# One of the eight shifted taps of the value tile's 3x3 convolution made by ScalarE and added by GpSimd, in a one-core Trainium2 block kernel

## The chip, the cores and the metric

The kernel runs on one core of one Trainium2 chip. The metric is the device time of one execution in microseconds (us). Three runs of the kernel before gave 1514.31, 1516.21 and 1516.56 us; the median is 1516.21 us.

Engines are named as in the profile: PE is TensorE's matmul, PEld its weight load, DVE is VectorE, ACT is ScalarE, POOL is GpSimd, SP is SyncE, whose queue issues the DMAs.

## What is computed

The block has two sub-layers on a latent stream of 1024 positions by 1024 channels (a grid of 16 rows by 64 columns). The first is a token mixer; the change does not touch it. The second is a convolutional feed-forward layer, and the change lies wholly in it:

```python
def dwconv2d(u, w, bias):
    c = u.shape[-1]
    y = lax.conv_general_dilated(u, w[:, :, None, :].astype(u.dtype), window_strides=(1, 1),
                                 padding="SAME", dimension_numbers=("NHWC", "HWIO", "NHWC"),
                                 feature_group_count=c)
    return y + bias

def conv_ffn(h, rows, w_up, conv_w, conv_b, w_down):
    b, n, _ = h.shape
    u = (h @ w_up).reshape(b, rows, n // rows, 2 * D_FF)
    u = dwconv2d(u, conv_w, conv_b).reshape(b, n, 2 * D_FF)
    gate, val = jnp.split(u, 2, axis=-1)
    return (jax.nn.gelu(gate) * val) @ w_down
```

D_FF is 2816, so the up-projection gives 22 tiles of 128 gate channels and 22 tiles of 128 value channels. Each channel is convolved over the grid with its own 3x3 weights: a centre tap and eight shifted taps.

## The kernel before

The order of the instructions on each engine is the order in which the program writes them; no scheduler changes it. Each engine works its own list in order, and semaphores make it wait for the others.

The feed-forward layer's first half is the loop of `ffn`, with one step for each n from 0 to 21. A step makes gate tile n and value tile n in PSUM, two tiles of 128x1024 called `ug` and `uv`, from seven products of half tiles (`up_product`, L1526, 12 matmuls of 128x512 each). The order of the products in step n is (n,0), then (n-1,6), then (n,1) to (n,5), so that a tile's last product, number 6, runs inside the next step. The four halves are the banks a0, a1 of `ug` and v0, v1 of `uv`. Between the products ScalarE moves banks (`copy`, L131): a0 to a1 after product 0 (`ug<-ug` in the profile), a1 to v0 after product 1 (`uv<-ug`), v1 to the buffer `p5` after product 3 (`p<-uv`), v0 to the buffer `u3` after product 5 (`u<-uv`). VectorE joins: a1 += p5 (`up_join` "g", L1542) and v1 += u3 (`up_join` "v", L1542, at the end of the step).

The convolution of a tile is `conv`: ScalarE writes the accumulator, centre tap and bias (L1552), and eight shifted taps are put in a queue. Each tap is one VectorE instruction (L1564) that reads the PSUM tile, multiplies with a weight per channel and adds into the accumulator in SBUF. Four of the eight taps (the corners) work on 15x63 = 945 elements, two on 960 and two on 1008. `up_conv(n-1, "v")` is called behind product (n-1,6), and the gate's behind join "g". VectorE's list for one step n is then: eight gate taps of tile n-1, five value taps of tile n-1, join "g" of n, three value taps of n-1, join "v" of n.

The weights of the next step are prepared in this step by `up_split`: ScalarE writes the rounded part (L131, `s<-s`), GpSimd the remainder (L138), one pair for each product. Splits 0 and 6 come first, then 1 and 2; behind split 2 GpSimd also makes a difference of weights (L1492), and then comes `glu(n-2)`, the product of gate and value tile (L1574), which is stored by DMA. Splits 3, 4 and 5, each with a sum of weights (L1474, L1476, L1478), end GpSimd's list of the step. ScalarE's list between splits 6 and 1 holds the value accumulator of tile n-1 and the copy `uv<-ug`.

`gate` (here `self.gp`) is a pool with four buffers of 128x512, tags `ghi`, `graw`, `glo` and `rb`. `p5` uses `ghi` and `graw` in turn, `u3` uses `glo` and `rb` in turn. After the loop, `down` does the down-projection (PE `dn`, L1795); the last tile's convolution lies in its first pass.

The loop's body, cut to the calls on which the steps below rest:

```python
for m, i in [(n, 0), (n - 1, 6)] + [(n, i) for i in range(1, 6)]:
    ...
                self.up_split(n + 1, i)
    ...
            if i == 0:
                self.taps(n - 1, "gt", 8)
            elif i == 6:
                self.up_conv(n - 1, "v")
            elif i == 2 and n > 1:
                self.glu(n - 2)
            elif i == 3:
                self.taps(n - 1, "vt", 5)
```

Of the kernel before, what the change touches and what calls it, by code (L numbers as in the profile page):

```python
# [8 lines left out]
F32 = mybir.dt.float32  # L9
F32R = mybir.dt.float32r  # L10
AF = mybir.ActivationFunctionType
OP = mybir.AluOpType
# [5 lines left out]
NP = FF // 128  # L18
# [94 lines left out]
class K:  # L113
# [1401 lines left out]
    def up_product(self, n, i):  # L1515
        nc, u = self.nc, self.U[n]
        name, form, b = self.PRODUCTS[i]
        w, (bh, bl) = u["w"].pop(name), self.B[form]
        o = self.bank(n, b)
        fresh = i in (0, 3)  # L1520
        for k in range(4):
            hi, lo = [w[:, j, k * 128:(k + 1) * 128] for j in range(2)]
            h, l = [x[k // 2][:, k % 2, :] for x in (bh, bl)]
            for m, (x, y) in enumerate(((hi, h), (hi, l), (lo, h))):
                first = fresh and k == 0 and m == 0
                nc.tensor.matmul(o, x, y, start=first, stop=k == 3 and m == 2, skip_group_check=not fresh)  # L1526
        self.sl.free(w)
        if i == 0:
            self.copy("act", self.bank(n, "a1"), o)
        elif i == 1:  # L1530
            self.copy("act", self.bank(n, "v0"), o)
        elif i == 3:
            u["p5"] = self.gp.tile([128, 512], F32, name="p5", tag=("ghi", "graw")[n % 2])
            self.copy("act", u["p5"], o)
        elif i == 5:
            u["u3"] = self.gp.tile([128, 512], F32, name="u3", tag=("glo", "rb")[n % 2])
            self.copy("act", u["u3"], o)

    def up_join(self, n, x):
# [3 lines left out]

    def up_conv(self, n, x):
        u = self.U[n]
        u[x + "a"], u[x + "t"] = self.conv(u[x], n if x == "g" else NP + n)

    def conv(self, ps, ti):

        nc = self.nc  # L1550
        acc = self.sl.get([128, S], any_=True)
        nc.scalar.activation(acc, ps, AF.Identity, bias=self.par["fcb"][:, ti:ti + 1], scale=self.fcw(4, ti))  # L1552
        a3 = acc.rearrange("p (y x) -> p y x", y=GH)
        p3 = ps.rearrange("p (y x) -> p y x", y=GH)
        taps = deque()
        for dy in (-1, 0, 1):
            for dx in (-1, 0, 1):
                if dy == 0 and dx == 0:
                    continue
                y0, y1, x0, x1 = max(0, -dy), GH - max(0, dy), max(0, -dx), GW - max(0, dx)  # L1560
                o = a3[:, y0:y1, x0:x1]
                i = p3[:, y0 + dy:y1 + dy, x0 + dx:x1 + dx]
                taps.append(lambda o=o, i=i, w=self.fcw((dy + 1) * 3 + dx + 1, ti):
                            nc.vector.scalar_tensor_tensor(o, i, w, o, op0=OP.mult, op1=OP.add))  # L1564
        return acc, taps

    def gelu(self, n):
        g = self.U[n]["ga"]
# [16 lines left out]
    def ffn(self):  # L1585
        sl = self.sl
        self.G = [self.dp.tile([128, 1024], F32, name=f"G{n}") for n in range(NP)]
        last = NP - 1

        todo = deque([(0, 4), (0, 5), (0, 6), (1, 1), (1, 3), (1, 4), (1, 5), (1, 6)])  # L1590
        self.down_plan()
        for n in range(NP):
            if n > 1:
                self.up_banks(n)
            if n + 2 < NP and n:
                self.up_load(n + 2)
            for m, i in [(n, 0), (n - 1, 6)] + [(n, i) for i in range(1, 6)]:
                if m >= 0 and not (n < 2 and i in (0, 2)):
                    if n == 0 or n == 1 and todo:
                        for _ in range(2 if n == 0 else 1):  # L1600
                            if todo:
                                self.up_split(*todo.popleft())
                    self.up_product(m, i)
                    if m == last:
                        self.up_free(i)
                if n == 0:
                    if i == 3:
                        self.up_load(2)
                    if i == 4:
                        self.up_join(0, "g")  # L1610
                        self.up_conv(0, "g")
                    continue
                if n + 1 < NP:
                    if n == 1 and i == 0:
                        self.up_sums(2)
                    self.up_split(n + 1, i)
                if n + 2 < NP and i in (3, 4, 5):
                    self.up_sums(n + 2, [i - 3])
                if i == 0:
                    self.taps(n - 1, "gt", 8)  # L1620
                elif i == 6:
                    self.up_conv(n - 1, "v")
                elif i == 2 and n > 1:
                    self.glu(n - 2)
                elif i == 3:
                    self.taps(n - 1, "vt", 5)
                elif i == 4:
                    self.gelu(n - 1)
                    self.up_join(n, "g")
                    self.up_conv(n, "g")  # L1630
                    self.taps(n - 1, "vt", 8)
            if n < last:
                self.up_join(n, "v")
        self.down()
# [362 lines left out]
```

## Time and profile before

| | |
|---|---|
| median of three runs | 1516.21 us |
| the profiled execution's own time | 1516.26 us |
| span of its trace | 1514.5 us |
| mean granted TensorE clock | 0.975 |
| PE busy | 1397.1 us (92%) |
| DVE busy | 1178.0 us (78%) |
| ACT busy | 668.7 us (44%) |
| POOL busy | 606.7 us (40%) |

The span is 1.8 us shorter than the profiled execution's own time. Busy shares are averages over stages that differ: the loop of `ffn` lies at 785 to 1275 us of the span, and its steady part is read in the rows below. In a timeline row the first number is the start in us from the span's start, the second the length, and the brackets hold the engine's idle time just before and what ended it.

### The profile page before, as it was taken

How to read it: one execution, taken by the hardware profiler on the slowest of the kernel's cores; microseconds unless marked ns; L12 is line 12 of the kernel's file. 1: busy time of each engine (PE TensorE's matmuls, PEld its weight loads, DVE VectorE, ACT ScalarE, POOL GpSimd, SP SyncE). 2: the span in 40 equal slices, each digit the busy share in tenths (PEclk: the TensorE clock that was granted, in tenths of full speed). 3: DMA queues.
4: the chain of work that ended last, by engine and by line, in shares of the span. 5: the costliest groups of instructions: out<-in, count | busy, mean ns of one | idle time of the engine just before them, and what ended most of it. 6: DMA issues, size and time to landing. Idle time of an engine off the chain costs nothing.

```text
span 1514.5 us, 16967 instructions
## 1 busy us (share of the span) xinstructions
PE 1397.1 (92%) x6333; PEld 1122.0 (74%) x6333; DVE 1178.0 (78%) x1347; ACT 668.7 (44%) x964; POOL 606.7 (40%) x422
## 2 busy tenths in 40 slices
PE   5999999998999689988995899999999999999994
PEld 3788888877888578877874677777777777788883
DVE  5768868767113988476567999999999999998696
ACT  6566677755110213332235444444444444545461
POOL 2221121122001443277057778777788775300000
PEclk9999999999999899999996999999999999999997
DMA  9310110101113445422431022211222208741642
GB/s 373 108 35 21 50 35 22 63 28 42 42 56 117 156 146 167 124 96 69 140 111 56 28 84 84 84 62 64 84 84 84 70 28 308 291 151 56 229 139 112
DMA packets 52787, 155.21 MB, mean 102 GB/s; under 512 B 5781, under 2 KB 10192, under 8 KB 52704
## 3 DMA queue, kind: packets, MB, share of 16 engines
q1 hardware_dynamic: 51264, 151.76, 28.7%
q10 hardware_dynamic: 1184, 2.11, 0.5%
q8 instruction: 50, 0.82, 0.2%
q14 instruction: 33, 0.27, 0.1%
q0 software_dynamic: 256, 0.25, 0.1%
HBM read 131.29 MB, written 22.81 MB: 102 GB/s over the span
## 4 chain that ended last, share of the span: by engine, by line
DVE 35%; PE 18%; issue 5%; ACT 1%; DMA 0%; DVEq 0%; ACTq 0%
DVE s L1564 24%; PE dn L1795 9%; PE big L194 6%; DVE s L138 2%; PE uv L1526 1%; PE ug L1526 1%; DVE ug L1542 1%; DVE uv L1542 1%; DVE s L1225 1%; DVE s L1787 1%; PE big L1212 0%; DVE s L1366 0%; DVE t L1367 0%; DVE s L338 0%; DVE s L1729 0%
## 5 line engine op out<-in xcount | busy, mean ns | idle before, releaser
L194 PE MATMUL big<-s,s 128*128 128x512 f32 (+2 forms) x2352 | 558.6, 396 | 9.0 <-DVE s L138 6.4
L194 PEld LDWEIGHTS big<-s,s 128*128 128x128 f32 (+2 forms) x2352 | 438.1, 189 | 114.2 <-DVE s L138 7.8
L138 POOL TENSOR_TENSOR s<-s,s 128x512 fp32r<-128x512 f32 (+1 forms) x229 | 351.3, 1551 | 273.2 <-ACT s L131 178.9
L131 ACT ACTIVATE s<-s 128x512 fp32r<-128x512 f32 (+2 forms) x406 | 264.4, 697 | 236.9 <-DVE mid L912 62.1
L1526 PE MATMUL ug<-s,s 128*128 128x512 f32 x1056 | 264.5, 399 | 24.3 <-ACT uv L131 13.4
L1526 PEld LDWEIGHTS ug<-s,s 128*128 128x128 f32 x1056 | 198.4, 190 | 79.5 <-ACT uv L131 22.0
L138 DVE TENSOR_TENSOR s<-s,s 128x512 fp32r<-128x512 f32 (+3 forms) x209 | 190.2, 940 | 74.3 <-ACT s L131 53.1
L1795 PE MATMUL dn<-s,s 128*128 128x512 f32 x924 | 216.3, 395 | 5.1 <-DVE s L138 4.0
L1564 DVE SCALAR_TENSOR_TENSOR s<-ug,rest,s 128x945 f32<-128x945 f32 (+2 forms) x176 | 214.9, 1221 | 5.4
L1564 DVE SCALAR_TENSOR_TENSOR s<-uv,rest,s 128x945 f32<-128x945 f32 (+2 forms) x176 | 214.7, 1220 | 4.7
L1526 PE MATMUL uv<-s,s 128*128 128x512 f32 x792 | 201.3, 404 | 11.3 <-DVE uv L1542 9.8
L1795 PEld LDWEIGHTS dn<-s,s 128*128 128x128 f32 x924 | 174.2, 189 | 46.9 <-DVE s L138 4.9
L1526 PEld LDWEIGHTS uv<-s,s 128*128 128x128 f32 x792 | 150.3, 192 | 54.8 <-DVE uv L1542 18.5
L782 POOL TENSOR_TENSOR s<-s,s 128x1280 f32<-128x1280 f32 x8 | 25.2, 3152 | 190.9 <-ACT s L778 190.9
L899 POOL TENSOR_TENSOR s<-s,s 128x1024 f32<-128x1024 f32 x8 | 21.1, 2642 | 127.4 <-PE big L194 120.7
L131 ACT ACTIVATE p<-uv 128x512 f32<-128x512 f32 x22 | 13.2, 600 | 106.2 <-PE uv L1526 106.2
L745 DVE SCALAR_TENSOR_TENSOR s<-big,par,s 128x1023 f32<-128x1023 f32 (+1 forms) x24 | 30.8, 1282 | 34.2 <-ACT s L742 33.6
L885 DVE TENSOR_TENSOR s<-big,s 128x1024 f32<-128x1024 f32 x8 | 9.8, 1223 | 61.1 <-PE big L194 61.1
L1574 POOL TENSOR_TENSOR s<-s,s 128x1024 f32<-128x1024 f32 x22 | 53.4, 2427 | 3.0 <-DVE s L1564 3.0
L1474 POOL TENSOR_TENSOR s<-s,s 128x512 f32<-128x512 f32 x22 | 28.6, 1299 | 63.5 <-DMA s<-in_ffn_w_up_b_dram 63.5
L1552 ACT ACTIVATE s<-uv,rest 128x1024 f32<-128x1024 f32 x22 | 26.6, 1208 | 47.6 <-POOL s L138 30.9
L777 ACT ACTIVATE s<-big,rest 128x1024 f32<-128x1024 f32 x32 | 35.7, 1117 | 24.6 <-PE big L194 17.8
(231 smaller groups left out, 1457.7 us busy)
## 6 DMA issues: line engine op xcount, KB each, us to landing
s<-in_mod_w_dram SPq DMA_DIRECT2D x48, 512.0 KB, 4.8
s<-in_ffn_w_up_b_dram SPq DMA_DIRECT2D x44, 512.0 KB, 4.4
s<-in_w_in_b_dram SPq DMA_DIRECT2D x32, 512.0 KB, 4.6
s<-G SPq DMA_DIRECT2D x55, 256.0 KB, 3.8
G<-s SPq DMA_DIRECT2D x22, 512.0 KB, 2.6
s<-in_ffn_w_down_dram SPq DMA_DIRECT2D x22, 512.0 KB, 7.1
s<-in_x_dram SPq DMA_DIRECT2D x16, 512.0 KB, 5.7
s<-G SPq DMA_DIRECT2D x11, 512.0 KB, 8.6
```

Of the source, the lines that this page charges most:

```text
L131: self.nc.scalar.activation(out, in_, AF.Copy)
L138: (self.nc.vector if eng == "dve" else self.nc.gpsimd).tensor_tensor(out, a, b, op=OP.subtract)
L194: return [lambda x=x: nc.tensor.matmul(x[0], x[1], x[2], start=x[3], stop=x[4]) for x in calls]
L745: nc.vector.scalar_tensor_tensor(u[:, lo:hi], z[:, lo + s:hi + s], tap[t], u[:, lo:hi], op0=OP.mult, op1=OP.add)
L777: nc.scalar.activation(lat, ps, AF.Sigmoid, bias=col)
L1474: p.tensor_tensor(u["x"][:, L], rg[:, L], rv[:, L], op=OP.subtract)
L1526: nc.tensor.matmul(o, x, y, start=first, stop=k == 3 and m == 2, skip_group_check=not fresh)
L1542: self.nc.vector.tensor_tensor(o, o, p, op=OP.add)
L1552: nc.scalar.activation(acc, ps, AF.Identity, bias=self.par["fcb"][:, ti:ti + 1], scale=self.fcw(4, ti))
L1564: nc.vector.scalar_tensor_tensor(o, i, w, o, op0=OP.mult, op1=OP.add))
L1574: nc.gpsimd.tensor_tensor(u["ga"], u["ga"], u["va"], op=OP.mult)
L1795: nc.tensor.matmul(bank[j], x, z, start=first and m == 0, stop=end and m == 2, skip_group_check=not check)
```

## The change

One of the eight value taps, the first corner (945 elements), leaves VectorE. In `conv`, for value tiles 0 to 20, ScalarE multiplies the shifted PSUM values with the tap's weight into two buffers `m` (8 rows of 63 = 504 elements and 7 rows of 63 = 441), right behind the accumulator. In `ffn`, at product (n,2), ahead of `glu(n-2)`, GpSimd adds the two buffers into the accumulator (L1635 in the changed file). VectorE's queue for the tile holds seven taps. The buffers `m` take the tags `graw` and `rb`; `p5` and `u3` keep one tag each. Tile 21 is not changed.

```diff
         elif i == 3:
-            u["p5"] = self.gp.tile([128, 512], F32, name="p5", tag=("ghi", "graw")[n % 2])
+            u["p5"] = self.gp.tile([128, 512], F32, name="p5", tag="ghi")
             self.copy("act", u["p5"], o)
         elif i == 5:
-            u["u3"] = self.gp.tile([128, 512], F32, name="u3", tag=("glo", "rb")[n % 2])
+            u["u3"] = self.gp.tile([128, 512], F32, name="u3", tag="glo")
             self.copy("act", u["u3"], o)
...
-        u[x + "a"], u[x + "t"] = self.conv(u[x], n if x == "g" else NP + n)
+        u[x + "a"], u[x + "t"], u[x + "r"] = self.conv(u[x], n if x == "g" else NP + n, x == "v" and n < NP - 1)
...
+                if shared and rest is None:
+                    rest = []
+                    h = (y1 - y0 + 1) // 2
+                    for tag, e in (("graw", slice(0, h)), ("rb", slice(h, y1 - y0))):
+                        m = self.gp.tile([128, 512], F32, name="m", tag=tag)
+                        m = m[:, 0:(min(e.stop, y1 - y0) - e.start) * (x1 - x0)].rearrange("p (y x) -> p y x", x=x1 - x0)
+                        nc.scalar.activation(m, i[:, e], AF.Copy, scale=self.fcw((dy + 1) * 3 + dx + 1, ti))
+                        rest.append((o[:, e], m))
+                    continue
...
-                elif i == 2 and n > 1:
-                    self.glu(n - 2)
+                elif i == 2:
+                    for o, m in self.U[n - 1]["vr"]:
+                        self.nc.gpsimd.tensor_tensor(o, o, m, op=OP.add)
+                    if n > 1:
+                        self.glu(n - 2)
```

GpSimd's list at product (n,2) of a step of the loop, before: two splits, the difference of weights, and the product of gate and value tile.

```order
L138 TENSOR_TENSOR s_6384<-s_6275,s_6384 128x512
L138 TENSOR_TENSOR s_6399<-s_6179,s_6399 128x512
L1492 TENSOR_TENSOR s_6179<-s_6179,s_6275 128x512
L1574 TENSOR_TENSOR s_6153<-s_6153,s_6222 128x1024
L138 TENSOR_TENSOR s_6419<-s_6181,s_6419 128x512
```

The same place with the change (line numbers are those of the changed file; `s_6384` is here the accumulator of value tile n-1):

```order
L138 TENSOR_TENSOR s_6403<-s_6291,s_6403 128x512
L138 TENSOR_TENSOR s_6418<-s_6189,s_6418 128x512
L1492 TENSOR_TENSOR s_6189<-s_6189,s_6291 128x512
L1635 TENSOR_TENSOR s_6384<-s_6384,m 128x8x63
L1635 TENSOR_TENSOR s_6384<-s_6384,m 128x7x63
L1584 TENSOR_TENSOR s_6164<-s_6164,s_6232 128x1024
L138 TENSOR_TENSOR s_6440<-s_6191,s_6440 128x512
```

The two adds stand behind the splits 1 and 2 and the difference of weights, and ahead of everything else of the step.

VectorE's list for the value taps of that tile, before, from the last gate tap of tile n-1 to the first gate tap of tile n:

```order
L1564 SCALAR_TENSOR_TENSOR s_6300<-ug,rest,s_6300 128x15x63
L1564 SCALAR_TENSOR_TENSOR s_6369<-uv,rest,s_6369 128x15x63
L1564 SCALAR_TENSOR_TENSOR s_6369<-uv,rest,s_6369 128x960
L1564 SCALAR_TENSOR_TENSOR s_6369<-uv,rest,s_6369 128x15x63
L1564 SCALAR_TENSOR_TENSOR s_6369<-uv,rest,s_6369 128x16x63 x2
L1542 TENSOR_TENSOR ug<-ug,p_6417 128x512
L1564 SCALAR_TENSOR_TENSOR s_6369<-uv,rest,s_6369 128x15x63
L1564 SCALAR_TENSOR_TENSOR s_6369<-uv,rest,s_6369 128x960
L1564 SCALAR_TENSOR_TENSOR s_6369<-uv,rest,s_6369 128x15x63
L1542 TENSOR_TENSOR uv<-uv,u_6464 128x512
L1564 SCALAR_TENSOR_TENSOR s_6447<-ug,rest,s_6447 128x15x63
```

And with the change:

```order
L1574 SCALAR_TENSOR_TENSOR s_6316<-ug,rest,s_6316 128x15x63
L1574 SCALAR_TENSOR_TENSOR s_6384<-uv,rest,s_6384 128x960
L1574 SCALAR_TENSOR_TENSOR s_6384<-uv,rest,s_6384 128x15x63
L1574 SCALAR_TENSOR_TENSOR s_6384<-uv,rest,s_6384 128x16x63 x2
L1574 SCALAR_TENSOR_TENSOR s_6384<-uv,rest,s_6384 128x15x63
L1542 TENSOR_TENSOR ug<-ug,p_6438 128x512
L1574 SCALAR_TENSOR_TENSOR s_6384<-uv,rest,s_6384 128x960
L1574 SCALAR_TENSOR_TENSOR s_6384<-uv,rest,s_6384 128x15x63
L1542 TENSOR_TENSOR uv<-uv,u_6484 128x512
L1574 SCALAR_TENSOR_TENSOR s_6468<-ug,rest,s_6468 128x15x63
```

The tap of 945 elements that stood first is gone; five value taps still stand ahead of join "g", two instead of three between the joins, and every one of them works on the accumulator into which GpSimd adds.

ScalarE's list around the copy `uv<-ug`, with the change:

```order
L1553 ACTIVATE s_6384<-uv,rest 128x1024
L1570 ACTIVATE m<-uv,rest 128x504
L1570 ACTIVATE m<-uv,rest 128x441
L131 ACTIVATE uv<-ug 128x512
L131 ACTIVATE s_6403<-s_6291 128x512
L131 ACTIVATE s_6418<-s_6189 128x512
```

The two rows L1570 are new; the others stand in the same order before.

## Rows read from the trace of the kernel before

**Rows 1.** The page, part 4: chain that ended last, shares by line.

```profile
DVE s L1564 24%; PE dn L1795 9%; PE big L194 6%; DVE s L138 2%; PE uv L1526 1%; PE ug L1526 1%; DVE ug L1542 1%; DVE uv L1542 1%; DVE s L1225 1%; DVE s L1787 1%; PE big L1212 0%; DVE s L1366 0%; DVE t L1367 0%; DVE s L338 0%; DVE s L1729 0%
```

**Rows 2.** Stretches: length; busy (x) of PE, PEld, DVE, ACT, POOL; granted clock; DMA.

```profile
1056.00:1076.90 20.90, 19.88 (x85) 15.62 (x84) 20.44 (x19) 9.36 (x14) 16.39 (x13) 1.00 0.21 76
```

**Rows 3.** Timeline of one step of the loop: VectorE.

```profile
1056.70 6.29 DVE L1564 SCALAR_TENSOR_TENSOR s<-uv,rest,s 128x945 f32<-128x945 f32 x5
1062.91 0.69 DVE L1542 TENSOR_TENSOR ug<-ug,p 128x512 f32<-128x512 f32 x1
1067.10 0.69 DVE L1542 TENSOR_TENSOR uv<-uv,u 128x512 f32<-128x512 f32 x1
1067.70 10.02 DVE L1564 SCALAR_TENSOR_TENSOR s<-ug,rest,s 128x945 f32<-128x945 f32 x8
```

**Rows 4.** The same step, in order of time: TensorE, ScalarE and GpSimd.

```profile
1056.59 1.29 POOL L1492 TENSOR_TENSOR s<-s,s 128x512 f32<-128x512 f32 x1
1057.84 2.42 POOL L1574 TENSOR_TENSOR s<-s,s 128x1024 f32<-128x1024 f32 x1
1059.30 0.60 ACT L131 ACTIVATE p<-uv 128x512 f32<-128x512 f32 x1 [4.90 <-PE uv L1526]
...
1067.85 3.06 PE L1526 MATMUL uv<-s,s 128*128 128x512 f32 x12 [0.35 <-DVE uv L1542]
1070.74 2.88 PE L1526 MATMUL ug<-s,s 128*128 128x512 f32 x12
1070.99 1.21 ACT L1552 ACTIVATE s<-uv,rest 128x1024 f32<-128x1024 f32 x1 [1.82 <-POOL s L138]
1073.66 0.58 ACT L131 ACTIVATE uv<-ug 128x512 f32<-128x512 f32 x1 [1.46 <-PE ug L1526]
1074.85 2.56 POOL L138 TENSOR_TENSOR s<-s,s 128x512 fp32r<-128x512 f32 x2 [3.57 <-ACT s L131]
1077.49 1.30 POOL L1492 TENSOR_TENSOR s<-s,s 128x512 f32<-128x512 f32 x1
```

**Rows 5.** Groups of 888 to 1265 us by form: busy, mean ns.

```profile
L1564 DVE SCALAR_TENSOR_TENSOR s<-uv,rest,s 128x945 f32<-128x945 f32 x72 | 86.2, 1197 | 1.3
L1574 POOL TENSOR_TENSOR s<-s,s 128x1024 f32<-128x1024 f32 x19 | 45.8, 2411 | 0.0
```

**Rows 6.** Timeline, joins "v" of tiles 1, 2 and 20.

```profile
855.83 0.69 DVE L1542 TENSOR_TENSOR uv<-uv,u 128x512 f32<-128x512 f32 x1
878.71 0.69 DVE L1542 TENSOR_TENSOR uv<-uv,u 128x512 f32<-128x512 f32 x1
1255.53 0.69 DVE L1542 TENSOR_TENSOR uv<-uv,u 128x512 f32<-128x512 f32 x1
```

**Rows 7.** Timeline of the loop's start: GpSimd and TensorE.

```profile
845.42 1.30 POOL L1492 TENSOR_TENSOR s<-s,s 128x512 f32<-128x512 f32 x1
856.58 5.49 PE L1526 MATMUL uv<-s,s 128*128 128x512 f32 x12 [3.04 <-DVE uv L1542]
861.86 3.27 PE L1526 MATMUL ug<-s,s 128*128 128x512 f32 x12
```

**Rows 8.** Timeline, TensorE behind shorter waits, in the stage before the loop.

```profile
667.94 1.78 PE L1212 MATMUL big<-s,s 126*128 126x512 f32 x4 [2.49 <-DVE s L1224]
676.89 1.05 PE L1212 MATMUL big<-s,s 126*128 126x512 f32 x4 [1.70 <-DVE s L1224]
```

**Rows 9.** Stretches behind three of those waits; columns as in rows 2.

```profile
667.90:671.30 3.40, 3.36 (x11) 3.02 (x12) 3.37 (x2) 1.31 (x3) 3.40 (x2) 0.51 0.00 0
676.90:681.60 4.70, 4.69 (x26) 3.82 (x26) 4.67 (x4) 0.38 (x1) 4.70 (x3) 1.00 0.42 124
856.60:862.00 5.40, 5.40 (x13) 4.24 (x14) 5.26 (x5) 0.00 (x0) 3.04 (x3) 0.50 0.00 0
```

**Rows 10.** Timeline: GpSimd ahead of the loop, and TensorE at its end.

```profile
799.21 8.47 POOL L138 TENSOR_TENSOR s<-s,s 128x512 fp32r<-128x512 f32 x5
...
1276.69 1.60 PE L1795 MATMUL dn<-s,s 128*128 128x512 f32 x6 [1.10 <-DVE s L1564]
```

More of the change, by code (lines that the diff above doesn't have):

```diff
@@ L1545, in up_conv, with conv @@
         u = self.U[n]
-        u[x + "a"], u[x + "t"] = self.conv(u[x], n if x == "g" else NP + n)
-    def conv(self, ps, ti):
+        u[x + "a"], u[x + "t"], u[x + "r"] = self.conv(u[x], n if x == "g" else NP + n, x == "v" and n < NP - 1)
+    def conv(self, ps, ti, shared=False):
         nc = self.nc
@@ L1554, in conv @@
         p3 = ps.rearrange("p (y x) -> p y x", y=GH)
-        taps = deque()
+        taps, rest = deque(), None
         for dy in (-1, 0, 1):
@@ L1562, in conv @@
                 i = p3[:, y0 + dy:y1 + dy, x0 + dx:x1 + dx]
+                if shared and rest is None:
[7 more added lines that the diff above has]
+                    continue
                 taps.append(lambda o=o, i=i, w=self.fcw((dy + 1) * 3 + dx + 1, ti):
                             nc.vector.scalar_tensor_tensor(o, i, w, o, op0=OP.mult, op1=OP.add))
-        return acc, taps
+        return acc, taps, rest
     def gelu(self, n):
```

## The prediction

> **What bounds the kernel now.** I began with the page's chain of work that ended last: the taps, L1564, hold 24% of the span, more than any other line [rows 1]. So the loop of the feed-forward layer is the place to read. The table of stretches shows one step of it: in 20.90 us VectorE is busy 20.44, TensorE 19.88, GpSimd 16.39, ScalarE 9.36, at the full granted clock [rows 2]. The joins "v" of tiles 2 and 20 lie 376.82 us apart, 18 steps, so a step takes 20.93 us [rows 6]. The timeline says who waits: VectorE's value taps, join "v" and gate taps follow each other without a stop [rows 3], while TensorE waits 0.35 us for join "v" before product (n,6) [rows 4]. Bare of that wait TensorE's step would be 20.58 us. So VectorE sets the step, and TensorE is right behind it.
>
> One more thing has to be read in those rows: a ring. Join "v" of tile n releases product (n,6): the join starts at 1067.10, the product at 1067.85 [rows 3, 4]. The same 0.75 us stands at the loop's start, from 855.83 to 856.58 [rows 6, 7], where the wait was 3.04 us; so this is a real dependence and not a label. Behind (n,6) comes product (n+1,1) at 1070.74, behind that ScalarE's copy `uv<-ug` at 1073.66, behind that two roundings of weights, which GpSimd awaits (idle 3.57 us) before splits 1 and 2 at 1074.85 and the difference of weights at 1077.49 [rows 4]. Before the change the ring ends there, since nothing that VectorE needs follows in GpSimd's list.
>
> **The change, part by part.** *The tap removed.* A tap of 945 elements takes 1.20 us [rows 5]. VectorE's step falls from 20.93 to 19.73 us, under TensorE's 20.58. Taken alone that would be worth 0.35 us a step, not 1.20.
>
> *ScalarE's two halves.* The nearest row is a copy of 512 elements out of PSUM, 0.60 us [rows 4]. Two of them behind the accumulator (1070.99 plus 1.21) end at 1073.40, ahead of the copy `uv<-ug` at 1073.66. I cost them at nothing: ScalarE's idle 1.46 us before that copy hides them, with 0.26 us to spare. Were that cover gone, each 0.1 us over it would lengthen the ring by as much.
>
> *The buffers.* `p5` and `u3` lose their second buffer, but each is read within some 4 us of being written (`p5` at 1059.30, join "g" at 1062.91 [rows 3, 4]) and written again a step later. No cost.
>
> *GpSimd's adds.* No row has them. GpSimd takes 1.30 us for 512 elements [rows 4] and 2.41 for 1024 [rows 5], so 0.19 us and 2.17 ns an element: 1.28 and 1.15 us for 504 and 441, of which the second starts 0.04 us early as neighbours there do: 2.39 us. The cheapest reading is 2.17 ns for 945 elements with no fixed part, 2.05; the dearest is GpSimd's slowest row near the loop, 8.47 us for five of 512, 1.69 each, 3.39 for both [rows 10]. I take 2.39, by the neighbours in the same list. GpSimd has the time: 16.39 and 2.39 make 18.78 us. The store of `glu` moves back by as much on GpSimd's list and SP's queue, and nothing in the loop reads it.
>
> *The wait that closes the ring.* The adds stand behind the difference of weights, and all seven value taps wait for them. From the copy `uv<-ug`: 1.19 us to split 1 and 2.64 to the difference (1073.66, 1074.85, 1077.49), 1.25 from it to the next instruction (1056.59 to 1057.84) [rows 4], adds 2.39, hand-over 0.06 (join "v" ends at 1067.79, the product starts at 1067.85): **7.53 us** to the first value tap. In the step shown the first value tap would be due 3.98 us after that copy (1056.70 plus 20.93, less 1073.66), so VectorE stands still for over 3 us. Then from the first value tap to join "v" 10.40 us less 1.20 for the tap [rows 3], 9.20; 0.75 to (n,6); 2.89 to (n+1,1); 2.92 to the next copy [rows 4]. The sum is **23.29 us** for one turn. A ring takes its own length, whatever the engines' busy time, so the step grows by 2.36 us, and TensorE's wait before (n,6) from 0.35 to 2.71 us.
>
> *What that wait does to TensorE's clock.* The rows show a wait of 2.49 us followed by 3.4 us at a granted clock of 0.51, and one of 3.04 by 5.4 us at 0.50, which is the 1.2 GHz level; after 1.70 us the clock stayed at 1.00 [rows 7 to 9]. 2.71 lies among the waits that fell, but these are single ones, and none shows that a wait repeated each step falls each time. Products (n,6) and (n+1,1) come right behind the wait and are in the ring, so what they lose is paid in full: 3.4 us at half speed cost 1.7; the stretch after 3.04 us cost 2.74 (5.28 and 3.27 in place of 2.89 and 2.92). I take 1.7, by the row nearest to 2.71, in two steps of three; the ends are none at all and 2.74 in each.
>
> **The sum.** *Start:* the difference of weights starts at 845.42 [rows 7]; plus 1.25, 2.39 and 0.06 the first value taps start at 849.12, join "v" of tile 1 at 858.32 (before 855.83), (1,6) at 859.07; with the low clock that stands there already, 5.28 and 3.27, the copy at 867.62, then 7.53 and 9.20: join "v" of tile 2 at 884.35 for 878.71, **+5.6**. *Tiles 2 to 20:* 18 turns of 2.36, **+42.5**. *End:* step 21 prepares no weights, so its adds come early; a tap less is worth the 1.10 us that TensorE waits there for the taps [rows 10], **-1.1**. *Clock:* 18 times two thirds of 1.7, **+20.4**. Together +67.4 on the profiled execution's 1516.26 (span 1514.5; the runs' median, 1516.21, is the same): **1583.7 us**.
>
> **Rivals.** *TensorE bounds.* If the adds came early enough or (n,6) did not wait for join "v", the freed VectorE would bring the step to 20.58: 18 times 0.35, 1.1 at the end and 1.2 at the start, 1507.7 us. The saturated VectorE speaks for it; against it stand the list, with three GpSimd instructions ahead of the adds, and the 0.75 us seen twice. It decides at once: with adds of 0.03 us the ring would already be as long as today's step (23.29 less 2.36). The Trainium skill (Perfetto Trace Analysis, section Optimizing Scalar/DVE Operations) says that with VectorE saturated, moving work to ScalarE or even GpSimd may make sense, though between VectorE and GpSimd it might not help because of a shared port; by its first half the time would be this rival's. The busy shares of rows 2 agree with its premise; the rule looks at load alone, and here the place of the wait decides.
>
> *The clock never falls.* The ring stands, 2.71 us is too little: 1563.3 us; with the cheapest adds 0.34 us less in each of 20 turns, 1556.5. For it: 1.70 us did nothing.
>
> *The clock falls in every step,* at 2.74: 47.0 plus 18 times 2.74, 1612.6 us. Dear adds (1.00 us more in 20 turns) would bring the forecast to 1603.7 and the wait to 3.7 us, where this rival is the rule.
>
> *Nothing moves,* because an unseen slack in ScalarE's or GpSimd's list lets the adds pass just in time: within 3 us of 1516. No row shows such slack.
>
> **How the numbers follow.** I give the forecast 0.50 (1565 to 1605), the ring without the clock 0.15, the low clock in every step or dear adds 0.22, TensorE as bound 0.09, no change 0.04. A measurement of this kernel can tell 0.2%, 3 us, from no change. So faster 0.09, same 0.04, slower 0.87. The range leaves out the two last cases: 1556, the cheapest adds without a clock loss, to 1620, the dear clock with adds a little over my price.
>
> **What would show it.** In the profile after, the first value taps should have an idle of over 3 us before them that GpSimd's add ended, TensorE's wait for join "v" should be 2.7 us or so in each step, the joins "v" 23.3 to 26 us apart, the adds 1.2 us each, and the granted clock under 1.00 in the loop. I am wrong if the value taps follow the gate taps without a stop, or if the step is 20.6 us.

## The result, and the profile after

The change makes the kernel slower: 1573.09 us (median of 5 runs, 1572.70 to 1575.14) against 1516.21 us (5 runs, 1514.31 to 1517.33), a ratio of 1.0381 with a 95% interval of 1.0368 to 1.0394. The forecast was 1583.7 us in a range of 1556 to 1620. The profiled execution took 1575.14 us; its span is 1573.4 us, 58.9 more than the span before.

The page of the kernel after, part 4, the chain that ended last, by engine and by line (L1574 is the tap, L1635 GpSimd's add, L1808 the down-projection):

```profile
PE 17%; DVE 16%; POOL 12%; issue 11%; ACT 3%; DMA 1%; SPq 0%; POOLq 0%; DVEq 0%; ACTq 0%
PE dn L1808 9%; POOL s L138 8%; DVE s L1574 7%; PE big L194 6%; POOL s L1635 3%; DVE s L138 2%; PE uv L1526 1%; PE ug L1526 1%; DVE ug L1542 1%; ACT s L131 1%; DVE s L1225 1%; ACT u L131 1%; ACT s L1553 1%; DVE s L1800 1%; DMA s<-in_ffn_w_down_dram 1%
```

Where the taps alone held 24% [rows 1], the chain now runs over all of VectorE, GpSimd, ScalarE and TensorE. One step of the loop in the table of stretches of the kernel after (columns as in rows 2), from join "v" of one tile to the next:

```profile
1099.20:1123.60 24.40, 21.24 (x84) 16.66 (x84) 19.41 (x19) 10.44 (x17) 18.35 (x14) 0.93 0.18 65
```

Nobody is busy throughout any more: VectorE 19.41 of 24.40 us, where it was 20.44 of 20.90 [rows 2]. The tap did leave VectorE, and the step shown is 3.5 us longer. The timeline of that step and the next one's start, kernel after, shows the ring:

```profile
1099.22 0.69 DVE L1542 TENSOR_TENSOR uv<-uv,u 128x512 f32<-128x512 f32 x1
...
1099.97 4.40 PE L1526 MATMUL uv<-s,s 128*128 128x512 f32 x12 [2.44 <-DVE uv L1542]
...
1104.20 2.88 PE L1526 MATMUL ug<-s,s 128*128 128x512 f32 x12
...
1107.12 0.58 ACT L131 ACTIVATE uv<-ug 128x512 f32<-128x512 f32 x1 [0.37 <-PE ug L1526]
...
1108.32 2.55 POOL L138 TENSOR_TENSOR s<-s,s 128x512 fp32r<-128x512 f32 x2 [4.04 <-ACT s L131]
...
1110.95 1.29 POOL L1492 TENSOR_TENSOR s<-s,s 128x512 f32<-128x512 f32 x1
1112.19 2.17 POOL L1635 TENSOR_TENSOR s<-s,m 128x504 f32<-128x504 f32 x2
...
1114.40 6.30 DVE L1574 SCALAR_TENSOR_TENSOR s<-uv,rest,s 128x960 f32<-128x960 f32 x5 [4.56 <-POOL s L1635]
...
1120.62 0.69 DVE L1542 TENSOR_TENSOR ug<-ug,p 128x512 f32<-128x512 f32 x1
...
1123.58 0.69 DVE L1542 TENSOR_TENSOR uv<-uv,u 128x512 f32<-128x512 f32 x1
...
1124.32 3.06 PE L1526 MATMUL uv<-s,s 128*128 128x512 f32 x12 [2.44 <-DVE uv L1542]
```

Join "v" releases product (n,6), that leads to (n+1,1), the copy, the splits, the difference of weights, the adds; VectorE has stood still for 4.56 us when the adds release the value taps, and 9.18 us later comes the next join "v". TensorE waits 2.44 us for it, where it waited 0.35 [rows 4]. The waits of 888 to 1300 us in the kernel after (us in total, times, longest) say the same for 17 steps:

```profile
DVE s L1574 <- POOL s L1635: 68.7, 17, 4.9
...
PE uv L1526 <- DVE uv L1542: 41.2, 17, 2.5
```

The two products behind the wait in the rows above differ: 4.40 us and 3.06. The stretches say why (same columns): the granted clock behind the first wait was 0.64 on the mean, so in part at the lower level of 1.2 GHz; behind the second it stayed at 1.00, the level of 2.4 GHz.

```profile
1099.90:1104.10 4.20, 4.13 (x12) 3.34 (x13) 4.09 (x5) 0.85 (x2) 4.20 (x4) 0.64 0.00 0
1124.30:1129.90 5.60, 5.58 (x24) 4.44 (x24) 5.46 (x5) 3.10 (x5) 4.37 (x4) 1.00 0.00 0
```

The joins "v" of tiles 2 and 20 in the timeline after, against those of rows 6:

```profile
884.35 0.69 DVE L1542 TENSOR_TENSOR uv<-uv,u 128x512 f32<-128x512 f32 x1
...
1314.18 0.69 DVE L1542 TENSOR_TENSOR uv<-uv,u 128x512 f32<-128x512 f32 x1
```

That is 429.83 us for 18 steps, 23.88 each, against 20.93: 53.0 of the 58.9 us. The 18 steps come in two kinds: eight of 22.98 to 23.10 us and ten of 24.36 to 24.66.

### The profile page after: what moved, and what is told of

Its sections match the earlier page's. It is cut to its first block, busy times and chain, and to the rows that moved or that the text cites. A ratio compares the mean times of both kernels' runs of the same rounds, so it can differ in the third digit from the quotient of the medians.

```text
span 1573.4 us, 17052 instructions
## 1 busy us (share of the span) xinstructions
PE 1414.7 (90%) x6333; PEld 1135.1 (72%) x6333; DVE 1154.6 (73%) x1326; ACT 690.7 (44%) x1006; POOL 649.0 (41%) x464
## 4 chain that ended last, share of the span: by engine, by line
PE 17%; DVE 16%; POOL 12%; issue 11%; ACT 3%; DMA 1%; SPq 0%; POOLq 0%; DVEq 0%; ACTq 0%
PE dn L1808 9%; POOL s L138 8%; DVE s L1574 7%; PE big L194 6%; POOL s L1635 3%; DVE s L138 2%; PE uv L1526 1%; PE ug L1526 1%; DVE ug L1542 1%; ACT s L131 1%; DVE s L1225 1%; ACT u L131 1%; ACT s L1553 1%; DVE s L1800 1%; DMA s<-in_ffn_w_down_dram 1%
## 5 line engine op out<-in xcount | busy, mean ns | idle before, releaser
L1526 PE MATMUL uv<-s,s 128*128 128x512 f32 x792 | 217.0, 427 | 54.2 <-DVE uv L1542 52.9
L1574 DVE SCALAR_TENSOR_TENSOR s<-uv,rest,s 128x945 f32<-128x945 f32 (+2 forms) x155 | 189.7, 1224 | 85.8 <-POOL s L1635 81.9
L1526 PEld LDWEIGHTS uv<-s,s 128*128 128x128 f32 x792 | 162.0, 207 | 102.0 <-DVE uv L1542 61.9
L1808 PE MATMUL dn<-s,s 128*128 128x512 f32 x924 | 216.2, 396 | 4.1 <-DVE s L138 4.1
L1574 DVE SCALAR_TENSOR_TENSOR s<-ug,rest,s 128x945 f32<-128x945 f32 (+2 forms) x176 | 215.0, 1221 | 5.4
L1808 PEld LDWEIGHTS dn<-s,s 128*128 128x128 f32 x924 | 174.3, 189 | 45.7 <-DVE s L138 5.1
L1553 ACT ACTIVATE s<-ug,rest 128x1024 f32<-128x1024 f32 x22 | 26.5, 1205 | 66.9 <-DVE ug L1542 66.9
L1584 POOL TENSOR_TENSOR s<-s,s 128x1024 f32<-128x1024 f32 x22 | 53.4, 2429 | 2.5 <-DVE s L1574 2.5
```

Of the source, the lines that this page charges most:

```text
L1584: nc.gpsimd.tensor_tensor(u["ga"], u["ga"], u["va"], op=OP.mult)
L1808: nc.tensor.matmul(bank[j], x, z, start=first and m == 0, stop=end and m == 2, skip_group_check=not check)
```

## The experiments

Each kernel is the changed one with the edit shown. The medians of before, measured beside them, were 1514 to 1516 us. A step is the mean of the 18 from join "v" of tile 2 to that of tile 20, read in the timeline as above.

**The adds moved ahead of the splits 1 and 2** (adds_at_6). Nothing else differs; the adds now stand where ScalarE's halves become ready.

```diff
                 elif i == 6:
                     self.up_conv(n - 1, "v")
-                elif i == 2:
                     for o, m in self.U[n - 1]["vr"]:
                         self.nc.gpsimd.tensor_tensor(o, o, m, op=OP.add)
-                    if n > 1:
-                        self.glu(n - 2)
+                elif i == 2 and n > 1:
+                    self.glu(n - 2)
```

> Same instructions as the change; GpSimd's two adds stand behind product (n,6) and the value accumulator, ahead of splits 1 and 2 and of the difference of weights. Ring theory: the adds then end before the eight gate taps do, the value taps do not wait, and the step goes to TensorE's 20.6 us: about 1508 us (1503 to 1513), faster than before, the wait of 3 to 5 us ahead of the value taps gone. Load theory (what costs is the work itself on ScalarE and GpSimd, or GpSimd and VectorE in each other's way): the same work is there, so about 1573 us stays.

Measured: 1500.32 us (4 runs, 1499.53 to 1502.35), a ratio to before of 0.9894 (0.9877 to 0.9910). That is 73 us off the change with the same instructions, and faster than the kernel before. It lies 2.7 us under the forecast range, mainly because TensorE's own step is shorter than the 20.6 us forecast. One step in its timeline:

```profile
1059.28 10.02 DVE L1574 SCALAR_TENSOR_TENSOR s<-ug,rest,s 128x945 f32<-128x945 f32 x8
...
1060.59 2.90 PE L1526 MATMUL uv<-s,s 128*128 128x512 f32 x12
...
1063.33 2.88 PE L1526 MATMUL ug<-s,s 128*128 128x512 f32 x12
...
1064.68 1.19 ACT L1570 ACTIVATE m<-uv,rest 128x504 f32<-128x504 f32 x2
1065.50 2.17 POOL L1634 TENSOR_TENSOR s<-s,m 128x504 f32<-128x504 f32 x2 [0.97 <-ACT m L1570]
1066.24 0.58 ACT L131 ACTIVATE uv<-ug 128x512 f32<-128x512 f32 x1 [0.37 <-PE ug L1526]
...
1069.21 6.29 DVE L1574 SCALAR_TENSOR_TENSOR s<-uv,rest,s 128x960 f32<-128x960 f32 x5
```

The adds end at 1067.67, the value taps start at 1069.21 behind the gate taps with no wait, and product (n,6) at 1060.59 waits for nobody. Its step is 20.35 us. The load theory is out: the place of the same work on the same engines makes a difference of 73 us. Nor do GpSimd and VectorE get in each other's way here: the two adds take 2.17 us beside VectorE's gate taps (1065.50), as they did in the change while VectorE stood still (1112.19), and the eight gate taps take 10.02 us, as they did before without adds beside them [rows 3].

**The halves made, not added** (m_no_adds).

```diff
-                elif i == 2:
-                    for o, m in self.U[n - 1]["vr"]:
-                        self.nc.gpsimd.tensor_tensor(o, o, m, op=OP.add)
-                    if n > 1:
-                        self.glu(n - 2)
+                elif i == 2 and n > 1:
+                    self.glu(n - 2)
```

> ScalarE makes the two halves, GpSimd does not add them (one tap of 21 value tiles is left out of the result). Ring theory: no adds, no ring: step 20.6 us, about 1508 us. If ScalarE's two rows lengthened the way from product (n,6) to the copy after product (n,1), the copy would start later than 5.81 us behind (n,6) and the time would stay above 1516 us.

Measured: 1500.57 us (2 runs, 1498.83 to 1502.32), step 20.34; the copy starts 5.66 us behind (n,6), not over 5.81. The adds at their better place cost nothing that these runs can tell from no adds at all. The forecast of 1508 us was too high for the same reason as above.

**Neither halves nor adds** (tap_left_out): as above, and the halves are not made.

```diff
-                    for tag, e in (("graw", slice(0, h)), ("rb", slice(h, y1 - y0))):
+                    for tag, e in ():
```

> Neither ScalarE's halves nor GpSimd's adds: the tap is left out of 21 value tiles. If ScalarE's two rows cost nothing, as forecast, this takes the same 1500 us as with the halves made and not added (within 3 us); if they cost, it is faster by more than 3 us.

Measured: 1499.91 us (2 runs, 1499.82 and 1499.99), step 20.32. That is 0.7 us under m_no_adds, inside its spread: ScalarE's two rows are free, as forecast.

**The gate tile's first tap left out as well** (both_taps_left_out): as tap_left_out, and

```diff
-        u[x + "a"], u[x + "t"], u[x + "r"] = self.conv(u[x], n if x == "g" else NP + n, x == "v" and n < NP - 1)
+        u[x + "a"], u[x + "t"], u[x + "r"] = self.conv(u[x], n if x == "g" else NP + n, n < NP - 1)
```

> The first tap is left out of 21 gate tiles as well as 21 value tiles, VectorE has 2.4 us less a step than before. If TensorE bounds the step once the ring is gone, the second tap is worth nothing: 1500 us (1497 to 1503) and the step stays 20.3 us. If VectorE still bounds it, a step falls by 1.2 us, to 19.1 or so, and the time to about 1476 us.

Measured: 1500.33 us (2 runs), step 20.34. A second tap off VectorE is worth nothing. One step in the table of stretches (VectorE is the third pair) and the line of the chain of 888 to 1240 us:

```profile
1050.00:1070.30 20.30, 19.63 (x86) 15.74 (x86) 18.15 (x17) 9.50 (x16) 16.43 (x12) 1.00 0.21 78
```

```profile
by line: PE ug L1526 55.9%; PE uv L1526 41.0%; ACT uv L131 2.8%; issue 0.3%
```

VectorE has 2 us to spare and the chain is TensorE's products with their wait for the copy `uv<-ug`. So 20.3 us is TensorE's floor, and a version of this idea that leaves TensorE's list as it is should stop near 1500 us.

**The adds one instruction later** (adds_after_glu).

```diff
                 elif i == 2:
+                    if n > 1:
+                        self.glu(n - 2)
                     for o, m in self.U[n - 1]["vr"]:
                         self.nc.gpsimd.tensor_tensor(o, o, m, op=OP.add)
-                    if n > 1:
-                        self.glu(n - 2)
```

> Same instructions as the change; the adds stand one instruction later, behind the product of gate and value tile (2.4 us). Ring theory: one turn grows from 23.0 to 25.4 us, TensorE's wait from 2.4 to 4.8 us, so that the clock falls in every step for 1.6 us or more: 27 us a step, about 1633 us (1615 to 1660). Load theory: the same work, about 1573 us.

Measured: 1636.18 us (2 runs), ratio 1.0791 (1.0770 to 1.0813), step 27.27. Timeline, and the loop in the table of stretches:

```profile
1091.84 6.30 DVE L1574 SCALAR_TENSOR_TENSOR s<-uv,rest,s 128x960 f32<-128x960 f32 x5 [7.50 <-POOL s L1637]
...
1101.76 4.94 PE L1526 MATMUL uv<-s,s 128*128 128x512 f32 x12 [4.77 <-DVE uv L1542]
```

```profile
890.00:1350.00 460.00, 367.38 (x1417) 286.27 (x1416) 325.74 (x288) 173.41 (x271) 310.43 (x237) 0.88 0.15 56
```

TensorE's wait grew from 2.44 to 4.77 us, the 2.4 us by which the adds moved, and now every step lies between 26.95 and 27.38 us: 23.0 and 2.4 for the ring, and the rest, 1.9, for the clock.

**One add of two** (one_add): the wait stays where it is, the adds are shorter.

```diff
-                    for o, m in self.U[n - 1]["vr"]:
+                    for o, m in self.U[n - 1]["vr"][:1]:
```

> Only the first of the two adds is done (the second half of one tap is left out of the result for 21 value tiles); place and wait stay. Ring theory: one turn is 1.0 us shorter, 22.0 us, TensorE waits 1.4 us, under the 1.7 us after which the clock stayed up: about 1538 us (1530 to 1546), granted clock 1.00 in the loop. If the clock fell as often as in the change, some 17 us more, 1555.

Measured: 1538.08 us (2 runs), ratio 1.0144 (1.0124 to 1.0165), step 22.04. Timeline, and the loop in the table of stretches:

```profile
1057.43 3.06 PE L1526 MATMUL uv<-s,s 128*128 128x512 f32 x12 [1.40 <-DVE uv L1542]
```

```profile
890.00:1250.00 360.00, 326.56 (x1377) 255.76 (x1376) 314.75 (x277) 168.97 (x260) 286.07 (x214) 1.00 0.20 72
```

The add left out takes 1.04 us, and the step is 1.0 us shorter than the change's short ones: a microsecond of GpSimd's time in the ring is a microsecond of every step. With waits of 1.38 to 1.47 us the clock stayed at 1.00. So two lengths of the ring are measured with the clock up, 22.0 and 23.0 us; the third, 25.4, is the 23.0 and the 2.4 us of the later place, since the clock was never up there. Behind their waits the clock fell in none of 18 steps, in ten, and in all.

**The ring cut short on VectorE** (join_early). The adds stay at the change's late place.

```diff
                 elif i == 3:
-                    self.taps(n - 1, "vt", 5)
+                    self.taps(n - 1, "vt", 3)
...
                     self.up_conv(n, "g")
-                    self.taps(n - 1, "vt", 8)
+                    self.taps(n - 1, "vt", 2)
             if n < last:
                 self.up_join(n, "v")
+            if n:
+                self.taps(n - 1, "vt", 8)
```

> GpSimd's adds stay at the change's late place; in VectorE's list two value taps move from ahead of join v to behind it (three taps, join g, two taps, join v, two taps). Ring theory: from the first value tap to join v 6.8 us in place of 9.2, one turn 20.6 us in place of 23.0, at TensorE's own step: about 1505 us (1500 to 1512), though the value taps still wait about 1 us for the late adds. If the lateness of the adds as such costs (VectorE's wait is lost time), VectorE's waits stay over 3 us and the time near 1573 us.

Measured: 1521.78 us (10 runs, 1519.49 to 1524.45), ratio 1.0043 (1.0031 to 1.0055). The ring did open: 51 us off the change, and the wait for the adds is 0.9 us. But the time missed its range by 10 us: the step is 21.08 us, and uneven, from 20.53 to 23.02. Two stretches of its timeline show a second ring behind the first:

```profile
1061.31 2.41 POOL L1584 TENSOR_TENSOR s<-s,s 128x1024 f32<-128x1024 f32 x1
...
1063.75 0.33 SPq L1586 DMA_DIRECT2D G<-s  x1
...
1066.53 1.21 ACT L1553 ACTIVATE s<-ug,rest 128x1024 f32<-128x1024 f32 x1 [1.20 <-DMA G<-s]
...
1067.64 0.58 ACT L131 ACTIVATE u<-uv 128x512 f32<-128x512 f32 x1
...
1068.26 0.70 DVE L1542 TENSOR_TENSOR uv<-uv,u 128x512 f32<-128x512 f32 x1
...
1084.48 0.33 SPq L1586 DMA_DIRECT2D G<-s  x1
...
1088.45 1.21 ACT L1553 ACTIVATE s<-ug,rest 128x1024 f32<-128x1024 f32 x1 [2.38 <-DMA G<-s]
...
1090.17 0.70 DVE L1542 TENSOR_TENSOR uv<-uv,u 128x512 f32<-128x512 f32 x1 [1.28 <-ACT u L131]
...
1090.92 3.07 PE L1526 MATMUL uv<-s,s 128*128 128x512 f32 x12 [1.33 <-DVE uv L1542]
```

The adds also push back the product of gate and value tile (L1584) and its store. The store frees a buffer, and ScalarE's accumulator of the next gate tile takes it, ahead of the copy to `u3`, which join "v" needs. From the copy `uv<-ug` at 1054.11 over these rows to the next one at 1074.82 it is 20.71 us, and what the store lands later is added to it, as in the second stretch. From 888 to 1240 us the 17 stores land after (minimum, median, maximum):

```profile
DMA to landing us min/median/max: 2.7/3.2/4.9
```

**The adds behind split 1** (adds_at_1): as the change, with the adds called at product (n,1).

```diff
-                elif i == 2:
+                elif i == 1:
                     for o, m in self.U[n - 1]["vr"]:
                         self.nc.gpsimd.tensor_tensor(o, o, m, op=OP.add)
-                    if n > 1:
-                        self.glu(n - 2)
+                elif i == 2 and n > 1:
+                    self.glu(n - 2)
```

> The adds stand behind split 1, ahead of split 2 and the difference of weights: 2.5 us earlier than in the change. Ring theory: one turn 23.0 less 2.5 is 20.5 us, just over the 20.34 us that TensorE takes by itself with the adds at product (n,6): 1500 to 1507 us, with the value taps waiting half a us or so.

Measured: 1516.71 us (8 runs, 1511.29 to 1518.73), ratio 1.0007 (0.9991 to 1.0024). Another miss to the same side: the step of the profiled execution (1511.29 us, the shortest of the eight) is 20.91 us, from 20.37 to 21.86, and ScalarE's accumulator waited for the store 17 times, up to 2.2 us. The product of gate and value tile stands at the same place of the list as in the change, so the second ring is as long as in join_early. The wait for the store does not by itself show that this ring bounds, because adds_at_6 has it as often and nearly as long. What differs is that here TensorE then waits for join "v", and in adds_at_6 no such wait is listed. The waits of 888 to 1240 us, adds_at_1 and then adds_at_6:

```profile
ACT s L1553 <- DMA G<-s: 23.3, 17, 2.2
...
PE uv L1526 <- DVE uv L1542: 4.9, 10, 1.2
```

```profile
ACT s L1553 <- DMA G<-s: 19.9, 17, 2.1
```

**The same, with the product of gate and value tile right behind the adds** (adds_glu_at_1), to test that reading.

```diff
                 elif i == 1:
                     for o, m in self.U[n - 1]["vr"]:
                         self.nc.gpsimd.tensor_tensor(o, o, m, op=OP.add)
-                elif i == 2 and n > 1:
-                    self.glu(n - 2)
+                    if n > 1:
+                        self.glu(n - 2)
```

> As adds_at_1, but the product of gate and value tile, and with it the DMA that stores it, stands right behind the adds, ahead of split 2 and the difference of weights (2.6 us earlier). Second-ring theory (product, store, the buffer it frees, ScalarE's next gate accumulator, the copy to u3, join v, and on to the adds: 20.7 us plus the store's scatter of 2.7 to 4.9 us): that ring falls to 18.2 us and has slack; the first ring at 20.5 us and TensorE's own 20.3 us remain: about 1503 us (1499 to 1507), with even steps. If adds_at_1 stood over its forecast for another cause, the time stays at 1511 to 1518 us with uneven steps.

Measured: 1504.83 us (4 runs, 1502.86 to 1505.83), ratio 0.9925 (0.9899 to 0.9951), step 20.42, all 18 between 20.35 and 20.48. In adds_at_1 the second ring was the cause: 12 us came back by moving one instruction, with its store, that no value tap waits for. For join_early the same reading rests on its timeline; this edit was not run there.

## Why the prediction was right

**What bounds, and the ring.** Both held. VectorE was the bound only by 0.6 us a step (20.93 against TensorE's floor of 20.35), and the adds closed a ring through all four engines. Of its sum of 23.29 us the rows after give 7.28 from the copy to the first value tap (7.53 forecast), 9.18 to join "v" (9.20), 0.74 to (n,6) (0.75), and, in the eight steps with the clock up, 5.77 to 5.90 from there to the next copy (5.81): some 23.0 us. The eight steps without a fall of the clock took 23.03 on the mean. The term that was mis-sized is GpSimd's adds: I took 1.28 and 1.15 us from its rows for 512 and 1024 elements, and the groups of the kernel after have them at

```profile
L1635 POOL TENSOR_TENSOR s<-s,m 128x504 f32<-128x504 f32 x17 | 19.9, 1173 | 0.0
L1635 POOL TENSOR_TENSOR s<-s,m 128x441 f32<-128x441 f32 x17 | 17.7, 1039 | 0.0
L1570 ACT ACTIVATE m<-uv,rest 128x504 f32<-128x504 f32 x18 | 12.1, 671 | 0.0
L1570 ACT ACTIVATE m<-uv,rest 128x441 f32<-128x441 f32 x18 | 11.4, 631 | 0.0
```

1.17 and 1.04: 0.2 us less a step, some 4 us in 18 steps, of the 10.6 by which the forecast was over the median.

**ScalarE's halves** take 0.67 and 0.63 us rather than 0.60, but both together 1.19 us in the rows above, and ScalarE still waits 0.37 us for TensorE before the copy, where the forecast had 0.26 to spare; tap_left_out shows them free.

**The store** of the product of gate and value tile was put at nothing because nothing in the loop reads it. For the change the result held, since the ring of the adds is longer. The reason did not: ScalarE waits for the buffer that the store frees, and in adds_at_1 that way cost 12 us.

**The clock** was forecast by the smallest of the waits that had been seen to fall [rows 7 to 9], as two steps of three at 1.7 us, 20.4 us. It was ten of 18 at 1.5 (24.56 less 23.03), 15 us, behind waits of 2.36 to 2.48 us and not the 2.71 forecast, so just under the shortest that had been seen to fall. Two thirds was a choice without a row behind it, and that it came so near is luck; that the clock falls in some steps and not in others behind the same wait of 2.4 us is what the kernel after shows. Adds_after_glu and one_add show both ends.

**Start and end.** The start cost 4.1 us (47.93 from join "v" of tile 0 to that of tile 2, for 43.81), not 5.6; the low clock behind tile 1's wait lasted shorter (from (1,6) to the next start 4.57 us, where it was 5.28), and the adds were quicker. That join "v" of tile 2 stands at 884.35, the very time forecast, is chance: 1.5 us of it lie ahead of the loop, where the two programs are alike. The end gained nothing where I gave it 1.1: TensorE no longer waits for the taps there, but behind join "v" of tile 20 the clock fell once more (4.28 us from (20,6) to the next start in place of 2.89), a cost that I had counted for the 18 turns alone. In sum, of the 58.9 us the turns of the ring make 37.8 (forecast 42.5), the clock in them 15.2 (20.4), the start 4.1 (5.6), the end 0.3 (-1.1), and the stretch ahead of the loop 1.5; the median, 1573.09, is 2 us under the profiled execution.

**The rivals.** TensorE as bound is what adds_at_6 shows, at 1500.3 and not 1507.7 us. Some 4 us of that is the step: I had taken TensorE's 20.93 us less its wait, 20.58; without the wait product (n,6) also takes 2.74 us to the next start in place of 2.89, and the step is 20.35. Another 2 us is the start (40.55 from join "v" of tile 0 to that of tile 2, 3.3 less than before, where I gave 1.2). The rule of the Trainium skill that was weighed (Perfetto Trace Analysis, section Optimizing Scalar/DVE Operations) says that work may move off a saturated VectorE. It agrees with adds_at_6, where the move gives 1% and TensorE's floor takes the rest of the tap's 1.2 us, and not with the change itself, at 1573.09 us. The rival without the clock, 1563.3 us, is what the eight short steps would give if all 18 were like them: some 1560 us (1575.14 less 15.2).

## What to carry to other kernels

Before work is moved to an engine that has time, follow the new wait round: which instruction stands ahead of the moved one in that engine's list, what releases that one, and whether the way leads back to the engine that now waits. If it does, and the ring is longer than the step that the busiest engine needs by itself, its length is the step, whatever the busy shares say, and the place in the list is worth more than the work (here 73 us for the same instructions, and in another version 12 us for a store that frees a buffer). Then see which engine bounds next, and how far below the present bound it lies, before counting the full duration of what was removed.

## What was not expected

A wait of the same length does not have the same price each time. Behind TensorE's waits of 2.36 to 2.48 us the clock fell in ten of 18 steps and stayed up in eight; behind 1.4 us it stayed up in all of one_add's steps, behind 4.7 to 4.8 it fell in all of adds_after_glu's. Nor does the longer wait always cost more. At the loop's start, behind join "v" of tile 1, it fell in adds_at_6 after 1.78 us and stayed up in adds_at_1 after 2.65. Timeline and stretch of adds_at_6, then of adds_at_1:

```profile
855.44 4.60 PE L1526 MATMUL uv<-s,s 128*128 128x512 f32 x12 [1.78 <-DVE uv L1542]
```

```profile
855.40:860.00 4.60, 4.56 (x13) 3.62 (x14) 4.49 (x4) 0.81 (x2) 4.35 (x4) 0.63 0.00 0
```

```profile
855.26 3.01 PE L1526 MATMUL uv<-s,s 128*128 128x512 f32 x12 [2.65 <-DVE uv L1542]
```

```profile
855.20:861.10 5.90, 5.81 (x24) 4.43 (x24) 5.76 (x6) 3.14 (x5) 4.41 (x4) 1.00 0.00 0
```

One_add's forecast leaned on a single wait of 1.70 us behind which the clock stayed up [rows 8, 9]; it came out at 1.4 us, but the runs show no length that parts the two cases. What decides a single step stays open. A product behind a wait also loses some 0.15 us with the clock up (2.89 for 2.74 us to the next start).

GpSimd's adds into the accumulator were quicker than its other adds and differences of that size: 1.17 us for 504 elements, where 512 took 1.29 to 1.31. What makes the difference was not tried.

The second ring, over the DMA store and the buffer that it frees, bounds nothing before or after the change (from 888 to 1240 us before, and to 1300 after, ScalarE's accumulator of the gate tile waits 17 times for join "g" and not for the store), and stands 0.4 us over TensorE's floor once the first is open. With it on the chain the scatter of the store's landing (2.7 to 4.9 us) shows as uneven steps.
